# Second attention of a two-layer encoder: values stationary, split probabilities moving, and one part buffer less

## The chip, the cores and the metric

The kernel runs on one core of a Trainium2 chip. The metric is the device time of one execution in microseconds (us). Before the change it was 1018.17 us, the median of three runs (1017.5, 1018.17 and 1019.22).

## What is computed

An encoder of two layers on a sequence of 256 tokens with 1024 features, all in fp32. Each layer is a half-weighted feed-forward, an attention and a second half-weighted feed-forward, with a norm ahead of and behind each:

```python
for i in range(DEPTH):
    g = norm_g[i]
    h = h + FFN_RES * _rmsnorm(_swiglu(_rmsnorm(h, g[0]), ffn1_wg[i], ffn1_wu[i], ffn1_wd[i]), g[1])
    u = _rmsnorm(h, g[2])
    m = _diff_attention(...) if i == 0 else _neighborhood_attention(u, na_w_in[j], na_w_out[j], na_rpb[j])
    h = h + _rmsnorm(m, g[3])
    h = h + FFN_RES * _rmsnorm(_swiglu(_rmsnorm(h, g[4]), ffn2_wg[i], ffn2_wu[i], ffn2_wd[i]), g[5])
```

The feed-forward is `(silu(x @ wg) * (x @ wu)) @ wd` with 2816 inner features. The second attention has 16 heads of 64 features; the tokens are a grid of 4 rows of 64, each query sees the 16 columns of its window in all four rows, and a learned bias is added to the scores before the softmax:

```python
sc = jnp.einsum('bqhd,brqjhd->bhqrj', q_row, k_win).astype(jnp.float32) * scale
sc = sc + bias.astype(jnp.float32)[None]
p = jax.nn.softmax(sc.reshape(b, nh, GRID_W, kh * kw), axis=-1)
return jnp.einsum('bhqrj,brqjhd->bqhd', p, v_win)
```

## The kernel before, in words

Most products are done in three parts: an fp32 number is split into a high part, rounded to the type float32r, and a low part, the rest; a product is high times high, high times low and low times high, added up in PSUM.

**Weights.** The weights come in parts of 128x1024 numbers through SyncE's queue into four raw buffers (L106). ACT writes the high part `whi` (L130) and DVE the low part `wlo` (L131), each in two pieces of 512 columns, into part buffers, of which there are nine for each kind (L35, L160). `W.get` (L138) splits up to four parts ahead of the one asked for, but no more than nine past the oldest part that is not yet released; `W.release` (L145) comes behind the last product that uses a part.

**Stages.** Six follow one another: feed-forward, first attention (`diff` true), feed-forward, feed-forward of layer 1, second attention (`diff` false), feed-forward. The 256 tokens are two halves, t = 0 and 1. A feed-forward begins with row products (`proj_rows`, L376: 16 matmuls at L380 and L381, which alternate between whi and wlo of the four parts, then eight at L383 with whi; tokens stationary, 512 weight columns moving), goes on with column products (`proj_col`, L405) and down projections (`row_steps`, L421), and ends with four pairs of down projections, eight parts, first for t = 0, then for t = 1. An attention ends with the output projection, eight parts too. Between the two halves of that end stand the norms of t = 0 (`norms`, L315), and the next stage's first products run while DVE, ACT and POOL do the norms of t = 1. Their result xg is transposed by PE, four 128x128 transposes for each half of the features, and split into xT (`norm_T`, L371). In every stage but the very first feed-forward, both halves are transposed behind the second row product (L528, L746).

**The second attention.** v is projected by rows (`v_rows`, L561) and kept in fp32; q and k are projected by rows and transposed (`qk_rows`, `qk_T`) or by columns (`qk_cols`, L607), and split. Everything comes in two groups g of eight heads, two query halves qh and two sets pr of four heads. `scores` (L623) makes the scores in two PSUM banks; `softmax` (L637) adds the bias on DVE (L652), takes the exponential on ACT (L661) and keeps 1/sum in `rz`. `probs_T` (L677) transposes the probabilities, 16 transposes for a g, qh and pr in two banks, and copies one bank with ACT (L684) and one with DVE (L686). `av` (L690) multiplies them by v in fp32: probabilities stationary, 64 columns of v moving (L702); DVE scales the result by `rz` (L710). `o_T` (L732) transposes that result and splits it into oT, which the output projection `wout` (L740) uses. The order of the calls is written out from L744 on; a scheduler then places the instructions on the engines, with a head start of 100 for `split_bank` (L349) and 200 for `norms`.

In PSUM there are four banks `acc`, two `mm` and two `tr`.

Of the kernel before, what the change touches and what calls it, by code (L numbers as in the profile page):

```python
# [34 lines left out]
PART_BUFS = 9  # L35
# [116 lines left out]
def encoder_kernel(ctx, tc, x, norm_g, f1g, f1u, f1d, f2g, f2u, f2d,  # L152
# [9 lines left out]
    l4p = ctx.enter_context(tc.tile_pool(name="l4p", bufs=6))  # L162
# [208 lines left out]
    def norm_T(xg, xT, t):  # L371
        for b in range(2):
            k = slice(4 * b, 4 * b + 4)
            transpose_split(xg[b], xT[0][:, t, k, :], xT[1][:, t, k, :])

    def proj_rows(ps, xT, t, keys):  # L376
        parts = [W.get(key) for key in keys]
        w = [(wh[:, j, :], wl[:, j, :]) for wh, wl in parts for j in range(wh.shape[1])]
        for kt, (wh, wl) in enumerate(w):
            nc.tensor.matmul(ps, xT[0][:, t, kt, :], wh, start=kt == 0, stop=False)  # L380
            nc.tensor.matmul(ps, xT[0][:, t, kt, :], wl, start=False, stop=False)  # L381
        for kt, (wh, wl) in enumerate(w):
            nc.tensor.matmul(ps, xT[1][:, t, kt, :], wh, start=False, stop=kt == KT - 1)  # L383
        if t == NH - 1:
            for key in keys:
                W.release(key)
# [84 lines left out]
    def ffn(key, li, gpre, xg1, xT, gpost, last, aside=None):  # L471
# [3 lines left out]
        def gu_rows(nme, t):  # L475
            ps = mm_tile()
            proj_rows(ps, xT, t, [(key, nme, 0, j) for j in range(KT * NC // UE)])
# [74 lines left out]
    def attn(key, li, gpre, xg1, xT, gpost):  # L552
# [8 lines left out]
        def v_rows(g, t):  # L561
            ps = mm_tile()
            proj_rows(ps, xT, t, keys_of(2, g))
            if t == 0:
                vv[g] = vp.tile([P, NH, NC], F32, tag="v", name=nm("v"))
            nc.scalar.activation(vv[g][:, t, :], ps, AF.Copy)
# [13 lines left out]
        def qk_rows(part, g, t):  # L580
            ps = mm_tile()
            proj_rows(ps, xT, t, keys_of(part, g))
# [54 lines left out]
        def softmax(g, qh, pr, banks):  # L637
# [26 lines left out]
            if diff:  # L664
# [7 lines left out]
                ps = ps[:1]  # L672
            steps[g, qh, pr] = ps, rz
# [3 lines left out]
        def probs_T(g, qh, pr):  # L677
            ps, rz = steps.pop((g, qh, pr))
            res = []
            for c, p in enumerate(ps):  # L680
# [8 lines left out]

        def av(g, qh):  # L690
            ob = bank(ps_tr, "tr")
            o = t2p.tile([P, NC], F32, tag="t2", name=nm("o"))
            e = P if diff else 64
            rzs = []
            for pr in range(2):
                aT, rz = aTs.pop((g, qh, pr))
                rzs.append(rz)
                for j in range(2):
                    for c in range(len(aT)):
                        hd = (2 * pr + j) if diff else (4 * pr + 2 * j + c)  # L700
# [4 lines left out]
                if not diff:  # L705
                    s = slice(pr * 256, (pr + 1) * 256)
                    l = [list(v_) for v_ in rz.ap]
                    rzb = bass.AP(tensor=rz.tensor, offset=rz.offset,
                                  ap=[l[0], [l[2][0], 2], [l[1][0], 2], [0, e]])
                    nc.vector.tensor_tensor(out=o[:, s].rearrange("p (j c e) -> p j c e", j=2, c=2),  # L710
                                            in0=ob[:, s].rearrange("p (j c e) -> p j c e", j=2, c=2),
                                            in1=rzb, op=ALU.mult)
            if diff:
                f = 1.0 - LAM_INIT
                ss = sm.tile([P, 4], F32, tag="ss4", name=nm("ss4"))
                for hd in range(4):
                    square(ob[:, hd * P:(hd + 1) * P], rzs[hd // 2][:, 0, hd % 2:hd % 2 + 1], ss[:, hd:hd + 1])
                ms = sm.tile([P, 4], F32, tag="ms", name=nm("sub"))
                nc.vector.tensor_scalar(out=ms, in0=ss, scalar1=1.0 / (P * f * f), scalar2=EPS / (f * f),
                                        op0=ALU.mult, op1=ALU.add)  # L720
                rs = sm.tile([P, 4], F32, tag="rs", name=nm("sub"))
                nc.gpsimd.tensor_tensor(out=rs, in0=ms, in1=mhalf, op=ALU.pow)
                for pr in range(2):
                    nc.vector.tensor_tensor(out=rs[:, 2 * pr:2 * pr + 2], in0=rs[:, 2 * pr:2 * pr + 2],
                                            in1=rzs[pr][:, 0, :], op=ALU.mult)
                for hd in range(4):
                    s = slice(hd * P, (hd + 1) * P)
                    nc.vector.scalar_tensor_tensor(out=o[:, s], in0=ob[:, s], scalar=rs[:, hd:hd + 1],
                                                   in1=subg, op0=ALU.mult, op1=ALU.mult)
            return o  # L730

        def o_T(g, qh, o):  # L732
            tr = transposes(o)
            hi, lo = [v[:, qh, 4 * g:4 * g + 4, :] for v in oT]
            if not diff:
                hi, lo, tr = [v.rearrange("p j (r q) -> p (j r) q", q=GRID_W) for v in (hi, lo, tr)]
                tr = flip(tr)
# [7 lines left out]
        qk_rows(0, 0, 0)  # L745
        norm_T(xg1, xT, 1)  # L746
# [25 lines left out]
        W.extra(len(W.extras))  # L772
        scores(0, 0, 0)
        scores(0, 0, 1)
        if diff:
            qk_rows(0, 1, 1)
            qk_T(0, 1, 0)
        else:
            qk_cols(0, 1)
        scores(0, 1, 0)  # L780
        probs_T(0, 0, 0)
        scores(0, 1, 1)
        probs_T(0, 0, 1)
        if not diff:
            queue_bias(1)
        o = av(0, 0)
        if diff:
# [4 lines left out]
        else:  # L792
            qk_cols(1, 1)
        o_T(0, 0, o)
        probs_T(0, 1, 0)
        probs_T(0, 1, 1)
        o = av(0, 1)
        if diff:
# [89 lines left out]
```

## Time and profile before

| | |
|---|---|
| timed runs, median | 1018.17 us |
| profiled execution | 1021.54 us |
| its span, first to last instruction | 1019.8 us |
| mean granted clock of TensorE | 0.997 of full speed |
| TensorE (PE) busy | 998.6 us, 98% |
| VectorE (DVE) busy | 661.4 us, 65% |
| ScalarE (ACT) busy | 579.1 us, 57% |
| GpSimd (POOL) busy | 22.9 us, 2% |
| HBM | 178 GB/s over the span |

Matmul records overlap, since they are pipelined: what a matmul costs PE is the distance from its start to the next one's start, not its duration. PEld is the load of the stationary operand, which runs beside the matmuls. The granted clock is 1.00 where TensorE has its full 2.4 GHz and 0.50 where it has 1.2 GHz.

### The profile page before, as it was taken

What the parts mean: (1) busy time and instruction counts of PE and PEld (TensorE: products, weight loads), DVE (VectorE), ACT (ScalarE), POOL (GpSimd) and SP (SyncE); (2) the same over time, 40 slices, a digit from 0 to 9 for tenths busy, and PEclk for the clock granted to TensorE, in tenths of its full rate; (3) what the DMA queues carried; (4) which work ended last, traced back from release to release, by engine and by line L of the source; (5) the groups of instructions that cost most, each with busy time, mean ns of one, the idle gap of its engine ahead of it and who ended that gap; (6) DMA issues with size and microseconds to landing.
All of it is one profiled execution on the core that took longest, in us unless ns stands there. A gap on an engine that the chain in (4) does not pass through costs nothing.

```text
span 1019.8 us, 14658 instructions
## 1 busy us (share of the span) xinstructions
PE 998.6 (98%) x5342; PEld 845.1 (83%) x5342; DVE 661.4 (65%) x1240; ACT 579.1 (57%) x1235; POOL 22.9 (2%) x38
## 2 busy tenths in 40 slices
PE   8899999999999999999999999999999999999997
PEld 5788888888777788888888888888898878888885
DVE  5666656577777666657576676657765477566562
ACT  6555555566776565555456555645755366555551
POOL 1000000000001000000000000000000010000000
PEclk9999999999999999999999999999999999999999
DMA  8866666375524766665377677546743446666631
GB/s 272 258 197 189 186 201 186 115 243 167 165 84 135 228 214 187 187 197 182 115 235 244 187 200 221 189 124 207 231 119 101 124 144 219 195 187 186 202 108 42
DMA packets 120825, 182.84 MB, mean 179 GB/s; under 512 B 5729, under 2 KB 87649, under 8 KB 120754
## 3 DMA queue, kind: packets, MB, share of 16 engines
q1 hardware_dynamic: 120608, 181.65, 57.6%
q8 instruction: 42, 0.69, 0.3%
q0 software_dynamic: 144, 0.26, 0.2%
q14 instruction: 29, 0.24, 0.1%
q10 hardware_dynamic: 2, 0.00, 0.0%
HBM read 180.84 MB, written 1.05 MB: 178 GB/s over the span
## 4 chain that ended last, share of the span: by engine, by line
PE 85%; DMA 4%; DVE 4%; ACT 4%; issue 1%; POOL 1%; SPq 0%; DVEq 0%; POOLq 0%; ACTq 0%
PE mm L413 25%; PE acc L438 24%; PE mm L415 13%; PE mm L380 5%; PE mm L381 5%; PE mm L383 4%; PE mm L438 2%; PE tr L702 2%; DVE wlo L131 2%; PE tr L365 2%; DMA raw<-in_ffn_wg_dram 2%; ACT whi L130 2%; DMA raw<-in_ffn_wu_dram 2%; DMA raw<-in_na_w_in_dram 1%; PE mm L397 1%
## 5 line engine op out<-in xcount | busy, mean ns | idle before, releaser
L131 DVE TENSOR_TENSOR wlo<-raw,whi 128x512 fp32r<-128x512 f32 x656 | 421.7, 686 | 201.5 <-ACT whi L130 114.4
L130 ACT ACTIVATE whi<-raw 128x512 fp32r<-128x512 f32 x656 | 365.6, 622 | 181.4 <-PE acc L438 51.2
L413 PE MATMUL mm<-xT,whi 128*128 128x512 f32 x1152 | 288.2, 392 | 0.7 <-DVE g L498 0.7
L413 PEld LDWEIGHTS mm<-xT,whi 128*128 128x128 f32 x1152 | 208.8, 189 | 40.1 <-DVE g L498 1.5
L438 PE MATMUL acc<-whi,hT 128*128 128x512 f32 x704 | 197.0, 391 | 0.0
L415 PEld LDWEIGHTS mm<-xT,wlo 128*128 128x128 f32 x1152 | 157.1, 190 | 11.3
L415 PE MATMUL mm<-xT,wlo 128*128 128x256 f32 x1152 | 160.6, 282 | 0.0
L438 PEld LDWEIGHTS acc<-whi,hT 128*128 128x128 f32 x704 | 130.3, 188 | 25.4
L380 PE MATMUL mm<-whi,xT 128*128 128x512 f32 x272 | 110.5, 406 | 3.7 <-ACT xT L355 3.4
L438 PE MATMUL acc<-wlo,hT 128*128 128x512 f32 x352 | 111.2, 390 | 0.0
L381 PE MATMUL mm<-wlo,xT 128*128 128x512 f32 x272 | 108.8, 400 | 0.1
L438 PEld LDWEIGHTS acc<-wlo,hT 128*128 128x128 f32 x352 | 66.1, 188 | 14.1
L383 PE MATMUL mm<-whi,xT 128*128 128x512 f32 x272 | 67.4, 390 | 0.0
L380 PEld LDWEIGHTS mm<-whi,xT 128*128 128x128 f32 x272 | 52.0, 191 | 16.8 <-ACT xT L355 6.0
L381 PEld LDWEIGHTS mm<-wlo,xT 128*128 128x128 f32 x272 | 51.9, 191 | 12.6 <-DVE wlo L131 2.6
L383 PEld LDWEIGHTS mm<-whi,xT 128*128 128x128 f32 x272 | 51.1, 188 | 10.6
L355 ACT ACTIVATE hT<-a 128x512 fp32r<-128x512 f32 x36 | 22.8, 633 | 63.7 <-DVE a L487 63.7
L498 DVE TENSOR_TENSOR u<-mm,u 128x256 f32<-128x256 f32 x72 | 30.4, 422 | 27.4 <-ACT u L497 27.2
L497 ACT ACTIVATE u<-mm 128x256 f32<-128x256 f32 x72 | 26.8, 373 | 29.6 <-PE mm L415 29.6
L497 ACT ACTIVATE g<-mm 128x256 f32<-128x256 f32 x72 | 26.7, 371 | 23.4 <-PE mm L415 23.4
L498 DVE TENSOR_TENSOR g<-mm,g 128x256 f32<-128x256 f32 x72 | 30.3, 420 | 10.2 <-ACT g L497 10.2
L330 DVE TENSOR_TENSOR yg<-acc,gain 128x512 f32<-128x512 f32 x20 | 13.7, 687 | 34.0 <-ACT junk L282 33.9
(113 smaller groups left out, 826.5 us busy)
## 6 DMA issues: line engine op xcount, KB each, us to landing
raw<-in_ffn_wg_dram SPq DMA_DIRECT2D x88, 512.0 KB, 4.6
raw<-in_ffn_wu_dram SPq DMA_DIRECT2D x88, 512.0 KB, 4.3
raw<-in_ffn_wd_dram SPq DMA_DIRECT2D x88, 512.0 KB, 4.0
raw<-in_diff_w_in_dram SPq DMA_DIRECT2D x24, 512.0 KB, 4.7
raw<-in_na_w_in_dram SPq DMA_DIRECT2D x24, 512.0 KB, 4.7
gain<-in_norm_g_dram SPq DMA_DIRECT2D x11, 512.0 KB, 5.1
raw<-in_diff_w_out_dram SPq DMA_DIRECT2D x8, 512.0 KB, 3.8
raw<-in_na_w_out_dram SPq DMA_DIRECT2D x8, 512.0 KB, 4.5
```

Source lines behind the costliest of these rows:

```text
L130: nc.scalar.activation(hi[:, e], raw[:, e], AF.Copy)
L131: nc.vector.tensor_tensor(out=lo[:, e], in0=raw[:, e], in1=hi.bitcast(F32)[:, e], op=ALU.subtract)
L355: last_act[0] = nc.scalar.activation(hi, ps, AF.Copy)
L365: nc.tensor.transpose(tr[:, j * P:(j + 1) * P], src[:, j * P:(j + 1) * P], ident)
L380: nc.tensor.matmul(ps, xT[0][:, t, kt, :], wh, start=kt == 0, stop=False)
L381: nc.tensor.matmul(ps, xT[0][:, t, kt, :], wl, start=False, stop=False)
L383: nc.tensor.matmul(ps, xT[1][:, t, kt, :], wh, start=False, stop=kt == KT - 1)
L413: nc.tensor.matmul(ps, wh, xT.both(kt), start=kt == 0, stop=False)
L415: nc.tensor.matmul(ps[:, S:], wl, xT.one(0, kt), start=False, stop=kt == KT - 1)
L438: nc.tensor.matmul(ys[b], (xh, xl)[xp](i), parts[i][wp][:, 0, HALVES[b]], start=first and b not in seen, stop=last and left[b] == 0)
L497: nc.scalar.activation(y[:, f], ps[:, S:], AF.Copy)
L498: nc.vector.tensor_tensor(out=y[:, f], in0=ps[:, :S], in1=y[:, f], op=ALU.add)
```

## The change

1. `PART_BUFS` goes from 9 to 8, and the pool `l4p`, which holds q, k, the split probabilities and the feed-forward's hidden parts, from 6 to 8 buffers.
2. `proj_rows` takes hooks: a function to call behind its n-th matmul. `while_rows` uses them to issue the first half of `norm_T` behind the 21st of 24 matmuls and the second half behind the 24th. This replaces the two halves behind the product in both attentions and in three feed-forwards.
3. In the second attention v is split into a high and a low part. The probabilities are scaled by 1/sum before they are transposed (32 instructions on DVE, 128x256), and the transposed ones are split, 16 banks, in the order of the mirrored columns. `av_cols` takes v as the stationary operand (64 columns) and the split probabilities of both query halves as the moving one (256 columns), 24 matmuls for each g and pr. The result has features on partitions and is split straight into oT; `o_T` and the scaling by `rz` fall away there. Its banks are of the kind `acc`.
4. The order of calls in the second attention is new: scores, transposes and values go by sets of heads, both query halves of a set behind one another.

```diff
-PART_BUFS = 9
+PART_BUFS = 8
...
-    l4p = ctx.enter_context(tc.tile_pool(name="l4p", bufs=6))
+    l4p = ctx.enter_context(tc.tile_pool(name="l4p", bufs=8))
...
+    def while_rows(xg, xT, t):
+
+        n = 3 * KT
+        return {n - 3: lambda: norm_T(xg, xT, t, [0]), n: lambda: norm_T(xg, xT, t, [1])}
+
+    def proj_rows(ps, xT, t, keys, hooks={}):
+
+        count = [0]
+
+        def product(*a, **k):
+            m = nc.tensor.matmul(*a, **k)
+            count[0] += 1
+            if count[0] in hooks:
+                with tc.issue_after(m.ins):
+                    hooks[count[0]]()
...
-            a0 = gated(gu_rows("u", 0), s0)
-            norm_T(xg1, xT, 1)
+            a0 = gated(gu_rows("u", 0, while_rows(xg1, xT, 1)), s0)
             s1 = act(gu_rows("g", 1))
...
+                vv[g] = [vp.tile([P, NH, NC], F32R, tag="v", name=nm("v")) for _ in range(2)]
+            split_bank(vv[g][0][:, t, :], vv[g][1][:, t, :], ps)
...
+            else:
+                for c in range(2):
+                    for j in range(2):
+                        nc.vector.tensor_scalar(out=ps[c][:, j, :], in0=ps[c][:, j, :],
+                                                scalar1=rz[:, c, j:j + 1], scalar2=None, op0=ALU.mult)
...
+            if not diff:
+                for c, p in enumerate(ps):
+                    if qh == 0:
+                        aTs[g, pr, c] = [l4p.tile([P, NH, 4, P], F32R, tag="l4", name=nm("aT")) for _ in range(2)]
+                    hi, lo = [v[:, qh].rearrange("p i (r q) -> p (i r) q", q=GRID_W) for v in aTs[g, pr, c]]
+                    tr = transposes(flat(p)).rearrange("p i (r q) -> p (i r) q", q=GRID_W)
+                    split_bank(hi, lo, flip(tr))
+                return
...
+        def av_cols(g, pr):
+
+            ob = [bank(ps_acc, "acc") for _ in range(2)]
+            aT = [aTs.pop((g, pr, c)) for c in range(2)]
+            vh, vl = vv[g]
+            for j in range(2):
+                for i, (w, a) in enumerate([(w, a) for w, a in ((vh, 0), (vh, 1), (vl, 0)) for _ in range(NH)]):
+                    kt = i % NH
+                    for c in range(2):
+                        hd = 4 * pr + 2 * j + c
+                        nc.tensor.matmul(ob[c][:64, j * S:(j + 1) * S],
+                                         w[:, kt, hd * 64:(hd + 1) * 64], aT[c][a][:, :, j * NH + kt, :],
+                                         start=i == 0, stop=i == 3 * NH - 1)
+            k = slice(4 * g + 2 * pr, 4 * g + 2 * pr + 2)
+            for c in range(2):
+                split_bank(*[v[c * 64:(c + 1) * 64, :, k, :].rearrange("p t k q -> p k t q") for v in oT],
+                           ob[c][:64].rearrange("p (k t q) -> p k t q", k=2, q=P))
...
-        qk_rows(0, 0, 0)
-        norm_T(xg1, xT, 1)
+        qk_rows(0, 0, 0, while_rows(xg1, xT, 1))
...
+        scores(0, 0, 0)
+        scores(0, 1, 0)
+        qk_cols(0, 1)
+        scores(0, 0, 1)
+        scores(0, 1, 1)
+        queue_bias(1)
+        probs_T(0, 0, 0)
+        probs_T(0, 1, 0)
+        qk_cols(1, 1)
+        av_cols(0, 0)
+        probs_T(0, 0, 1)
+        probs_T(0, 1, 1)
+        W.extra(len(W.extras))
+        scores(1, 0, 0)
+        scores(1, 1, 0)
+        av_cols(0, 1)
+        v_rows(1, 0)
+        scores(1, 0, 1)
+        scores(1, 1, 1)
+        v_rows(1, 1)
+        y0 = [mm_tile() for _ in range(2)]
+        probs_T(1, 0, 0)
+        probs_T(1, 1, 0)
+        wout(y0, 0, [0, 1, 2, 3])
+        av_cols(1, 0)
+        probs_T(1, 0, 1)
+        probs_T(1, 1, 1)
+        wout(y0, 0, [4, 5])
+        av_cols(1, 1)
```

Three pieces of the order follow. In the names, the number behind `whi`, `wlo` and `raw` is that of the part; parts 234 to 237 are those of the second row product of the second attention, and lines of the changed kernel are counted in its own file.

DVE, from layer 1's first feed-forward into the second attention, before:

```order
L131 TENSOR_TENSOR wlo236_6818<-raw236_6749,whi236_6817 128x512 x2
L131 TENSOR_TENSOR wlo237_6826<-raw237_6757,whi237_6825 128x512
L294 SCALAR_TENSOR_TENSOR pre_569_6787<-ss2_568_6782 128x1
L131 TENSOR_TENSOR wlo237_6826<-raw237_6757,whi237_6825 128x512
L307 SCALAR_TENSOR_TENSOR xg_571_6791<-h1_92,pre_570_6789,gain_447_5021 128x512
L307 SCALAR_TENSOR_TENSOR xg_572_6793<-h1_92,pre_570_6789,gain_447_5021 128x512
L131 TENSOR_TENSOR wlo238_6861<-raw238_6807,whi238_6860 128x512 x2
```

and of the changed kernel:

```order
L131 TENSOR_TENSOR wlo235_6810<-raw235_6715,whi235_6809 128x512 x2
L131 TENSOR_TENSOR wlo236_6818<-raw236_6749,whi236_6817 128x512
L294 SCALAR_TENSOR_TENSOR pre_569_6787<-ss2_568_6782 128x1
L131 TENSOR_TENSOR wlo236_6818<-raw236_6749,whi236_6817 128x512
L307 SCALAR_TENSOR_TENSOR xg_571_6791<-h1_92,pre_570_6789,gain_447_5021 128x512
L307 SCALAR_TENSOR_TENSOR xg_572_6793<-h1_92,pre_570_6789,gain_447_5021 128x512
L356 TENSOR_TENSOR v_578_6858<-mm_576_6800,v_577_6857 128x512
L131 TENSOR_TENSOR wlo237_6826<-raw237_6757,whi237_6825 128x512 x2
```

Part 236 has the place that part 237 had, and part 237 that of part 238, behind both xg; the low part of v is new ahead of it.

PE at the end of the same row product, where before the rows L365 stood behind all eight of the last matmuls; changed kernel:

```order
L386 MATMUL mm_579_6861<-wlo237_6826,xT_560_6676 128x512
L386 MATMUL mm_579_6861<-whi234_6801,xT_560_6676 128x512 x2
L386 MATMUL mm_579_6861<-whi235_6809,xT_560_6676 128x512 x2
L386 MATMUL mm_579_6861<-whi236_6817,xT_560_6676 128x512
L365 MATMUL tr_580_6883<-ident_116,xg_571_6791 128x128 x4
L386 MATMUL mm_579_6861<-whi236_6817,xT_560_6676 128x512
L386 MATMUL mm_579_6861<-whi237_6825,xT_560_6676 128x512 x2
L365 MATMUL tr_581_6893<-ident_116,xg_572_6793 128x128 x4
```

The first set of transposes of xg moved ahead of the product's last three matmuls.

PE where the first products with the values of the changed kernel's second set of heads end and the next row product begins:

```order
L732 MATMUL acc_670_7722<-aT_646_7621,v_577_6857 64x256 x2
L732 MATMUL acc_670_7722<-aT_647_7622,v_577_6857 64x256 x2
L732 MATMUL acc_670_7722<-aT_646_7621,v_578_6858 64x256 x2
L732 MATMUL acc_670_7722<-aT_646_7621,v_577_6857 64x256 x2
L732 MATMUL acc_670_7722<-aT_647_7622,v_577_6857 64x256 x2
L732 MATMUL acc_670_7722<-aT_646_7621,v_578_6858 64x256 x2
L386 MATMUL mm_672_7752<-whi250_7451,xT_560_6676 128x512
```

Here `v_577` and `v_578` are the high and the low part of v, `aT_646` and `aT_647` those of the probabilities; before, L702 had the fp32 probabilities and v here, with 64 columns to a matmul.

## Rows read from the trace of the kernel before

**Rows 1.** The page, part 1: busy us, share of the span, instructions.

```profile
PE 998.6 (98%) x5342; PEld 845.1 (83%) x5342; DVE 661.4 (65%) x1240; ACT 579.1 (57%) x1235; POOL 22.9 (2%) x38
```

**Rows 2.** Waits of PE and PEld, whole span: us in total, times, longest.

```profile
PE mm L380 <- ACT xT L355: 3.4, 6, 2.1
...
PE acc L632 <- ACT qk L355: 0.8, 1, 0.8
...
PE acc L633 <- DVE qk L356: 0.5, 1, 0.5
...
PEld mm L381 <- DVE wlo L131: 2.6, 7, 0.5
```

**Rows 3.** Timeline into the first attention: start us, us, engine, line, operation, count.

```profile
211.60 0.39 PE L381 MATMUL mm<-wlo,xT 128*128 128x512 f32 x1
...
211.82 1.98 PE L383 MATMUL mm<-whi,xT 128*128 128x512 f32 x8
212.96 1.28 DVE L131 TENSOR_TENSOR wlo<-raw,whi 128x512 fp32r<-128x512 f32 x2
...
213.64 1.04 PE L365 MATMUL tr<-ident,xg 128*128 128x128 f32 x8
...
214.98 0.50 PE L380 MATMUL mm<-whi,xT 128*128 128x512 f32 x1 [0.30 <-ACT xT L355]
```

**Rows 4.** Timeline of PE, second attention, transposes of nat between two products.

```profile
713.12 0.60 PE L365 MATMUL tr<-ident,nat 128*128 128x128 f32 x4
713.47 0.48 PE L380 MATMUL mm<-whi,xT 128*128 128x512 f32 x1
713.78 0.39 PE L381 MATMUL mm<-wlo,xT 128*128 128x512 f32 x1
```

**Rows 5.** Timeline, into the second feed-forward.

```profile
331.24 1.89 DVE L131 TENSOR_TENSOR wlo<-raw,whi 128x512 fp32r<-128x512 f32 x3
...
331.98 0.50 PE L381 MATMUL mm<-wlo,xT 128*128 128x512 f32 x1
```

**Rows 6.** Timeline, into layer 1.

```profile
518.22 0.39 PE L381 MATMUL mm<-wlo,xT 128*128 128x512 f32 x1
...
519.35 1.29 DVE L131 TENSOR_TENSOR wlo<-raw,whi 128x512 fp32r<-128x512 f32 x2
```

**Rows 7.** Timeline, into the second attention.

```profile
704.02 0.50 PE L381 MATMUL mm<-wlo,xT 128*128 128x512 f32 x1
...
705.74 1.28 DVE L131 TENSOR_TENSOR wlo<-raw,whi 128x512 fp32r<-128x512 f32 x2
```

**Rows 8.** Timeline, into the last feed-forward.

```profile
834.84 2.49 DVE L131 TENSOR_TENSOR wlo<-raw,whi 128x512 fp32r<-128x512 f32 x4
...
836.18 0.50 PE L381 MATMUL mm<-wlo,xT 128*128 128x512 f32 x1
```

**Rows 9.** Timeline of PE, second attention's end: its first and last rows.

```profile
730.54 0.60 PE L365 MATMUL tr<-ident,nat 128*128 128x128 f32 x4
...
827.07 0.40 PE L380 MATMUL mm<-whi,xT 128*128 128x512 f32 x1
```

**Rows 10.** Timeline of PE, second attention: q and k projection by columns, values.

```profile
754.24 0.28 PE L398 MATMUL mm<-xT,whi 128*128 128x256 f32 x1
754.36 0.28 PE L399 MATMUL mm<-xT,wlo 128*128 128x256 f32 x1
754.50 2.00 PE L702 MATMUL tr<-v,aT 128*128 128x64 f32 x16
756.31 0.36 PE L397 MATMUL mm<-xT,whi 128*128 128x256 f32 x1
```

**Rows 11.** Windows: length, busy PE, PEld, DVE, ACT, POOL; then PEclk, DMA, GB/s.

```profile
33.00:36.00 3.00, 0.40 (x3) 0.05 (x1) 2.00 (x4) 2.30 (x4) 0.00 (x0) 1.00 0.78 269
734.00:738.00 4.00, 4.00 (x26) 3.78 (x25) 3.83 (x20) 3.51 (x9) 0.00 (x0) 0.57 0.38 135
730.00:827.00 97.00, 94.16 (x658) 82.40 (x658) 58.94 (x156) 53.83 (x138) 1.42 (x2) 0.98 0.38 115
```

More of the change, by code (lines that the diff above doesn't have):

```diff
@@ L379, in proj_rows @@
         for kt, (wh, wl) in enumerate(w):
-            nc.tensor.matmul(ps, xT[0][:, t, kt, :], wh, start=kt == 0, stop=False)
-            nc.tensor.matmul(ps, xT[0][:, t, kt, :], wl, start=False, stop=False)
+            product(ps, xT[0][:, t, kt, :], wh, start=kt == 0, stop=False)
+            product(ps, xT[0][:, t, kt, :], wl, start=False, stop=False)
         for kt, (wh, wl) in enumerate(w):
-            nc.tensor.matmul(ps, xT[1][:, t, kt, :], wh, start=False, stop=kt == KT - 1)
+            product(ps, xT[1][:, t, kt, :], wh, start=False, stop=kt == KT - 1)
         if t == NH - 1:
@@ L473, in ffn, with gu_rows @@
         hT = {}
-        def gu_rows(nme, t):
+        def gu_rows(nme, t, hooks={}):
             ps = mm_tile()
-            proj_rows(ps, xT, t, [(key, nme, 0, j) for j in range(KT * NC // UE)])
+            proj_rows(ps, xT, t, [(key, nme, 0, j) for j in range(KT * NC // UE)], hooks)
             return ps
@@ L692, in av @@
             o = t2p.tile([P, NC], F32, tag="t2", name=nm("o"))
[L693 removed]
+            e = P
             rzs = []
@@ L704, in av @@
                                              start=kt == 0, stop=kt == NH - 1)
[L705 to L729, printed above, removed]
+            f = 1.0 - LAM_INIT
@@ new lines, in av @@
+            ss = sm.tile([P, 4], F32, tag="ss4", name=nm("ss4"))
+            for hd in range(4):
+                square(ob[:, hd * P:(hd + 1) * P], rzs[hd // 2][:, 0, hd % 2:hd % 2 + 1], ss[:, hd:hd + 1])
+            ms = sm.tile([P, 4], F32, tag="ms", name=nm("sub"))
+            nc.vector.tensor_scalar(out=ms, in0=ss, scalar1=1.0 / (P * f * f), scalar2=EPS / (f * f),
+                                    op0=ALU.mult, op1=ALU.add)
+            rs = sm.tile([P, 4], F32, tag="rs", name=nm("sub"))
@@ new lines, in av @@
+            nc.gpsimd.tensor_tensor(out=rs, in0=ms, in1=mhalf, op=ALU.pow)
+            for pr in range(2):
+                nc.vector.tensor_tensor(out=rs[:, 2 * pr:2 * pr + 2], in0=rs[:, 2 * pr:2 * pr + 2],
+                                        in1=rzs[pr][:, 0, :], op=ALU.mult)
+            for hd in range(4):
+                s = slice(hd * P, (hd + 1) * P)
+                nc.vector.scalar_tensor_tensor(out=o[:, s], in0=ob[:, s], scalar=rs[:, hd:hd + 1],
+                                               in1=subg, op0=ALU.mult, op1=ALU.mult)
@@ new lines, in attn @@
+            wout(y0, 0, [0, 1, 2, 3])
+            probs_T(1, 0, 0)
+            probs_T(1, 0, 1)
+            o = av(1, 0)
+            y1 = [bank(ps_acc, "acc") for _ in range(2)]
+            wout(y1, 1, [0, 1])
+            probs_T(1, 1, 0)
+            probs_T(1, 1, 1)
+            o_T(1, 0, o)
+            o = av(1, 1)
+            wout(y0, 0, [4, 5])
+            wout(y0, 0, [6, 7])
+            xg = norms(0, y0, gpost, gpre, False)
+            o_T(1, 1, o)
+            wout(y1, 1, [2, 3])
@@ L795, in attn @@
+            wout(y1, 1, [4, 5, 6])
+            nxT = xt_tiles("xT")
+            norm_T(xg, nxT, 0)
+            wout(y1, 1, [7])
+            xg = norms(1, y1, gpost, gpre, False)
+            return xg, nxT
+        W.extra(len(W.extras))
+        scores(0, 0, 0)
+        scores(0, 1, 0)
+        qk_cols(0, 1)
+        scores(0, 0, 1)
+        scores(0, 1, 1)
+        queue_bias(1)
+        probs_T(0, 0, 0)
         probs_T(0, 1, 0)
+        qk_cols(1, 1)
+        av_cols(0, 0)
+        probs_T(0, 0, 1)
```

65 lines of the change are left out of this document (23 added, 42 removed).

## The prediction, made before the changed kernel ran

> **What bounds the kernel now.** I read the page's busy times first, then the list of what TensorE waits for, then the timeline around each place that the change touches. PE is busy for 998.6 us, 98% of the span [rows 1], and the longest entry among its waits is 3.4 us in total [rows 2]. So the time is PE's own stream: a microsecond that PE is spared, or waits, is one of the run, and DVE (65%) and ACT (57%) matter only where PE arrives before their result. I therefore go along PE's stream and ask what gets shorter and what comes late. The profiled execution took 1021.54 us, the timed runs have a median of 1018.17; differences are worked out in the trace and put on the median. Under 0.2%, about 2 us, a measurement of this kernel cannot be told from no change.
>
> **Transposes inside a product (a gain).** At five places PE did both sets of transposes of xg behind the product and then waited for ACT's split. At the first, the product ends at 213.64 and the next begins at 214.98: 1.34 us [rows 3]; the other four show the same rows with 1.29 or 1.34, together 6.55 us. Now the first set stands three matmuls ahead of the product's end, and its split runs beside those. Eight 512-column matmuls take 211.82 to 213.64, 0.23 us each [rows 3]. One set between matmuls, with the slower first matmul behind it, takes from 713.12 to 713.78 [rows 4]; less that matmul's 0.23, a set costs 0.43 us. Two sets at five places make 4.3 us, a gain of 6.55 - 4.3 = **2.2 us**. The wait for the split, 0.30 us in the row of 214.98, goes in any case, so at least 1.4 us.
>
> **Nine part buffers to eight (a loss).** A feed-forward and an attention end with eight parts held to their last products. With nine buffers one part of the next stage could be split ahead of them; with eight none can. The order on DVE shows what that does: around the boundary each part's wlo stands where the following part's stood. Raw loads shift alike, since a raw buffer comes free with its split. So I take the time at which the following part's second half was done, and compare it with the start of the matmul that needs the part last with wlo, the sixteenth of the stage's second product:
> - into the first attention, wlo ends at 212.96 + 1.28 = 214.24, that matmul stood at 211.60: 2.6 us [rows 3];
> - into the feed-forward behind it, 331.24 + 1.89 = 333.13 against 331.98: 1.2 us [rows 5];
> - into layer 1, 519.35 + 1.29 = 520.64 against 518.22: 2.4 us [rows 6];
> - into the second attention, 705.74 + 1.28 = 707.02 against 704.02, and the new split of v with 0.6 us (half of the 1.28 for two wlo) stands ahead of it: 3.6 us [rows 7];
> - into the last feed-forward, 834.84 + 2.49 = 837.33 against 836.18: 1.2 us [rows 8].
>
> In sum **11.0 us**. The reason is that wlo of the product's last part is now queued behind both xg of the norm, which in the trace it preceded. Behind the waiting matmul PE has only its own next products, whose parts are then ready, so nothing is lost twice. Elsewhere the trace shows reserve: PE's weight loads wait for a wlo at L381 alone, seven times and 2.6 us in all [rows 2], and never in the column products or the down projections. There I put the loss of a buffer at nothing; the cover is parts split ahead, and if it is gone, each late part costs up to one half split, 0.6 us. Ends: 8 us, if two of the smaller places turn out covered, and 13 us, if ACT's half, also shifted, is late on top.
>
> **The end of the second attention (a gain).** From the transposes of nat at 730.54 to the next stage's first product at 827.07 it takes 96.5 us [rows 9].
> - Values: 128 records with 64 columns, 16 of them from 754.50 to 756.31, 0.11 each: some 14.2 us. In their place come 96 matmuls with 256 moving columns; the nearest rows, 256 columns of the same class of operands, are 0.12 us apart (754.24, 754.36) [rows 10]: 11.5 us. Ends: 0.11, the record replaced, and 0.23, the 512-column step [rows 3]: 10.6 to 22 us. I stay at 0.12, since the columns are the same number. Gain 2.7.
> - Four sets of transposes of o go: 4 x 0.43 = 1.7 us.
> - Clock: from 734 to 738 the granted clock was 0.57, so half speed for most of it: 4 x 0.43 = 1.7 us lost [rows 11], right behind PE's waits for qk of 0.8 and 0.5 us [rows 2]. Before that place stand now 19 matmuls whose data are done, 12 of scores and 7 of the next projection, so I take the 1.7 us as gained.
> - Waits: 0.8 and 0.5 for qk [rows 2], and some shorter ones for aT. After: the scores of the second query half need q's second half, split in the same places of ACT and DVE as what PE waited for before, so the same 1.3 us; and where the scores of group 1 begin, two splits of oT and two of aT stand on DVE ahead of a bank that the next transposes need, some 1.0 us. I put the difference at 0.
> - Smaller pieces of PE's time between kinds of work: the values' matmuls were cut into the projections in pieces (754.36, 754.50 and 756.31 are such changes [rows 10]), o's transposes into other products. Each such change costs some 0.08 us, which is what the set of transposes shows, 0.31 us from 713.47 to 713.78 for a matmul of 0.23 [rows 4], and some 20 go: 1.6 us.
>
> Together 2.7 + 1.7 + 1.7 + 1.6 = **7.7 us**. What hides the rest: 32 new scalings of 128x256, 16 splits of p in place of 8 copies, four of v and four more of oT keep DVE busy for some 16 us more, at 0.3 us for 256 columns and 0.6 for 512 by the same pair of wlo, less 3 us for eight scalings that go. DVE had 58.9 us in 97 [rows 11] and gets about 75 in 89: still covered, except in bursts such as the 1.0 us above. Ends: 4.5 us, with 3.5 us more of such waits, and 10.5 with none.
>
> **Sum.** -2.2 + 11.0 - 7.7 = +1.1 us: 1018.17 + 1.1, rounded **1019.0 us**, no change.
>
> **Rivals.**
> - *Slower: the clock falls at the boundaries.* PE's waits there come in pieces with two matmuls between, as ahead of 734. Against it: the 3 us from 33 to 36, with 0.40 us of PE work in them, kept the clock at 1.00 [rows 11]. If each of the three long waits (2.4 to 3.6 us) costs 1.7 us, as from 734 to 738, that is 5.1: 1024.1 us. It decides from one fall on: 1019.0 + 1.7 = 1020.7 us. The Trainium skill, "TensorE: Matmul & The Clock Gate", Part 1, says that the gate follows how busy PE has recently been and that half speed is the state after idleness; by that rule each boundary wait is a candidate. The fall behind 734 agrees with it, the stretch from 33 to 36 does not. Chance 0.22.
> - *Slower: DVE fills up.* With 4.5 in place of 7.7 us from the attention's end: 1022.5 us. For it: the 75 of 89 us. Against: most of it lies beside the projections of q and k, which ask nothing of DVE. Chance 0.10.
> - *Faster: the buffers cost half.* If the scheduled place is not what bounds wlo, because parts that stood later in the order were simply not wanted earlier, 11.0 becomes 4 to 6: 1012 to 1014 us. Against: DVE works its queue in order, and xg ahead of the part are bound by the norm. Chance 0.24. If eight buffers cost nothing, so that the change only does its other parts: 1018.2 - 9.9 = 1008 us, chance 0.08.
>
> **How the numbers follow.** The forecast, within 2 us of no change, has 0.36, faster 0.24 + 0.08 = 0.32, slower 0.22 + 0.10 = 0.32. All losses high and gains low give 1018.2 - 1.4 + 13 - 4.5 = 1025.3; with a fall of the clock beside it the range reaches 1026. Losses low and gains high give 1013.5; half-price buffers with the best gains reach 1010. Range 1010 to 1026.
>
> **What would show it.** In the second product of each stage the last matmuls with wlo should wait for DVE, by 2.6, 1.2, 2.4, 3.6 and 1.2 us more than before; without these waits the buffer term is wrong. Behind that product no more than 0.5 us should stand until the next. The values' matmuls should be 0.12 us apart. From the transposes of nat to the next stage some 89 us should stand in place of 96.5. A clock under 1.00 behind a boundary would be the first rival, more than 5 us of waits of PE for aT, oT or p from DVE the second.

## The result, and the profile after

| | before | after |
|---|---|---|
| timed runs, median of 8 each | 1018.91 us | 1024.24 us |
| ratio, with its 95% interval | | 1.0057, 1.0042 to 1.0072 |
| profiled execution | 1021.54 us | 1024.0 us |
| its span | 1019.8 us | 1022.2 us |

The kernel became slower by 0.57%, 5.8 us by the ratio (the two medians lie 5.3 us apart), where the prediction had 1019.0 us, no change, as the likeliest outcome. The time lies inside the stated range of 1010 to 1026 us, at the place of its first rival. PE does less and still ends later: the page's first part, after, to be held against [rows 1]:

```profile
PE 994.6 (97%) x5294; PEld 839.8 (82%) x5294; DVE 676.6 (66%) x1280; ACT 586.3 (57%) x1247; POOL 22.6 (2%) x38
```

PE has 4 us less of busy time, and more waits. The waits of PE and PEld over the whole span (us in total, times, longest), after, to be held against [rows 2]; lines 380 and 381 of the old file are L386 here:

```profile
PE mm L386 <- DVE wlo L131: 8.1, 6, 2.3
PE mm L386 <- ACT xT L355: 2.1, 2, 1.9
...
PE tr L365 <- DVE aT L356: 1.5, 2, 0.8
...
PE acc L651 <- ACT qk L355: 0.8, 1, 0.8
PE mm L453 <- DVE v L356: 0.8, 1, 0.8
...
PE mm L453 <- ACT oT L355: 0.3, 1, 0.3
```

```profile
PEld mm L386 <- DVE wlo L131: 16.0, 23, 2.8
```

The wait of the weight loads for wlo grew from 2.6 us [rows 2] to 16.0. In the matmuls themselves it is 8.1 us, where the kernel before shows no wait of a matmul for wlo over 0.15 us in these places. The five boundaries have one long one each. Timeline of PE after, start and length in us, with the idle time before it in brackets; in order into the first attention, the second feed-forward, layer 1, the second attention and the last feed-forward:

```profile
212.03 0.50 PE L386 MATMUL mm<-wlo,xT 128*128 128x512 f32 x1 [1.72 <-DVE wlo L131]
...
332.17 0.50 PE L386 MATMUL mm<-wlo,xT 128*128 128x512 f32 x1 [0.54 <-DVE wlo L131]
...
521.64 0.64 PE L386 MATMUL mm<-wlo,xT 128*128 128x512 f32 x1 [1.73 <-DVE wlo L131]
...
712.13 0.50 PE L386 MATMUL mm<-wlo,xT 128*128 128x512 f32 x1 [2.32 <-DVE wlo L131]
...
839.12 0.50 PE L386 MATMUL mm<-wlo,xT 128*128 128x512 f32 x1 [1.59 <-DVE wlo L131]
```

In four of them it is the fourteenth matmul of the product that waits, in the second feed-forward the twelfth: the first half of the product's last part (there the half before it) came late already, not only the second half, which the sixteenth needs and which the prediction looked at. Matmuls near the wait also stand 0.33 us apart in place of 0.23:

```profile
212.63 0.50 PE L386 MATMUL mm<-wlo,xT 128*128 128x512 f32 x1
212.96 1.32 PE L386 MATMUL mm<-whi,xT 128*128 128x512 f32 x5
```

Into the second attention the wait is 0.6 us longer than into the first; there the new split of v stands on DVE between xg and wlo:

```profile
709.46 1.41 DVE L307 SCALAR_TENSOR_TENSOR xg<-h,pre,gain 128x512 f32<-128x512 f32 x2 [0.45 <-POOL pre L297]
710.79 0.68 DVE L356 TENSOR_TENSOR v<-mm,v 128x512 fp32r<-128x512 f32 x1
711.39 1.28 DVE L131 TENSOR_TENSOR wlo<-raw,whi 128x512 fp32r<-128x512 f32 x2
```

The row at 521.64 differs in its length, 0.64 us against 0.50: there the clock has fallen. Windows after (length, busy PE, PEld, DVE, ACT, POOL; then granted clock, DMA share, GB/s), all of 5 us up to PE's last matmul whose clock is under 0.985:

```profile
520.00:525.00 5.00, 3.36 (x8) 2.48 (x9) 2.19 (x4) 0.00 (x0) 0.00 (x0) 0.69 0.91 295
525.00:530.00 5.00, 5.00 (x27) 4.17 (x26) 1.89 (x3) 1.20 (x2) 0.00 (x0) 0.97 0.30 102
...
710.00:715.00 5.00, 2.87 (x8) 2.09 (x9) 2.67 (x5) 0.00 (x0) 0.00 (x0) 0.80 0.81 260
715.00:720.00 5.00, 5.00 (x25) 4.16 (x24) 1.38 (x2) 1.68 (x3) 0.00 (x0) 0.86 0.30 107
```

A clock of 0.69 over 5 us is 5 x 0.31 = 1.55 us lost, with 0.15 in the next window 1.7 in all; the second pair gives 1.0 + 0.7 = 1.7. These are two falls, both behind a boundary's wait, of the three that the first rival spoke of.

To see where all of the time lies, I cut PE's timeline of each run at the same places: for a boundary, from the first matmul of the next stage's first product to the first of its third, which holds the wait, the transposes and any fall of the clock. In us, profiled executions:

| boundary into | before | after | less the fall | change | predicted (wait less 0.44 of hooks) |
|---|---|---|---|---|---|
| first attention | 12.22 | 14.33 | 14.33 | +2.1 | 2.6 - 0.44 = +2.2 |
| second feed-forward | 12.71 | 12.96 | 12.96 | +0.25 | 1.2 - 0.44 = +0.8 |
| layer 1 | 12.17 | 16.09 | 14.4 | +2.2 | 2.4 - 0.44 = +2.0 |
| second attention | 12.50 | 17.06 | 15.4 | +2.9 | 3.6 - 0.44 = +3.2 |
| last feed-forward | 12.58 | 13.73 | 13.73 | +1.15 | 1.2 - 0.44 = +0.8 |
| sum | 62.18 | 74.17 | 70.8 | +8.6 | +8.8 |

The rest of the second attention, from its third product to its end, went from 119.53 to 111.68 us, 7.85 less (predicted 7.7). Part of that is chance: the execution before had a fall of the clock in this stretch, 1.7 us, that is no work of the change (below). The stretch, after, is shown by its first and last rows, to be held against [rows 9]:

```profile
740.28 0.60 PE L365 MATMUL tr<-ident,nat 128*128 128x128 f32 x4
...
828.98 0.39 PE L386 MATMUL mm<-whi,xT 128*128 128x512 f32 x1
```

The last stage is 0.6 us shorter behind its boundary, and the other stretches changed by less than 0.3 us each, but for the start: the first stage took 202.76 us before and 201.27 after, and between 199.5 and 203.8 in all the runs below, in no order of buffers or hooks; in three of them a fall of the clock is in it. What sets the rest of it was not looked into. So the two spans differ by only 2.5 us; with the fall (1.7) and the longer start (1.5) of the execution before set aside it is 5.7, near the timed 5.8.

The end of the second attention, windows (same columns, to be held against the last of [rows 11]) and groups by line (engine, operation, out<-in, count, busy us, mean ns, idle before), after:

```profile
740.00:829.00 89.00, 85.50 (x609) 75.82 (x608) 72.50 (x192) 59.22 (x147) 1.10 (x2) 1.00 0.37 117
```

```profile
L732 PE MATMUL acc<-aT,v 128*64 128x256 f32 x96 | 11.9, 278 | 0.0
L671 DVE CUSTOM_DVE_ANT_0 p<-acc,bias 128x256 f32<-128x256 f32 x32 | 11.9, 418 | 0.0
...
L356 DVE TENSOR_TENSOR aT<-tr,aT 128x512 fp32r<-128x512 f32 x16 | 10.7, 687 | 1.6 <-ACT aT L355 1.3
...
L695 DVE TENSOR_SCALAR p<-p,rz 128x256 f32<-128x256 f32 x32 | 9.1, 349 | 0.2
...
L356 DVE TENSOR_TENSOR oT<-acc,oT 64x512 fp32r<-64x512 f32 x8 | 5.5, 683 | 5.5 <-ACT oT L355 5.3
```

DVE is busy for 72.5 of 89 us, near the forecast's 75, and PE waits for it only twice for aT and once for v, 2.3 us in all: the second rival did not come. All waits of PE in the stretch, 2.6 us before, are 3.4 after; the forecast had no difference. The clock is 1.00 throughout.

### The profile page after: what moved, and what is told of

It is laid out like the page before. It is cut to its first block, busy times and chain, and to the rows that moved or that the text cites. A ratio compares the mean times of both kernels' runs of the same rounds, so it can differ in the third digit from the quotient of the medians.

```text
span 1022.2 us, 14601 instructions
## 1 busy us (share of the span) xinstructions
PE 994.6 (97%) x5294; PEld 839.8 (82%) x5294; DVE 676.6 (66%) x1280; ACT 586.3 (57%) x1247; POOL 22.6 (2%) x38
## 4 chain that ended last, share of the span: by engine, by line
PE 79%; DVE 7%; DMA 5%; ACT 5%; issue 3%; POOL 1%; SPq 0%; POOLq 0%; DVEq 0%; ACTq 0%
PE mm L428 26%; PE acc L453 21%; PE mm L430 13%; PE mm L386 11%; DVE wlo L131 3%; DMA raw<-in_ffn_wu_dram 3%; PE mm L453 2%; PE tr L365 2%; ACT whi L130 2%; ACT junk L282 1%; ACT p L680 1%; PE acc L732 1%; PE tr L752 1%; POOL pre L297 1%; PE mm L413 1%
## 5 line engine op out<-in xcount | busy, mean ns | idle before, releaser
L386 PE MATMUL mm<-whi,xT 128*128 128x512 f32 x544 | 180.2, 404 | 2.2 <-ACT xT L355 2.1
L386 PEld LDWEIGHTS mm<-whi,xT 128*128 128x128 f32 x544 | 104.4, 193 | 23.8 <-ACT xT L355 3.3
L386 PE MATMUL mm<-wlo,xT 128*128 128x512 f32 x272 | 110.8, 407 | 8.1 <-DVE wlo L131 8.1
L386 PEld LDWEIGHTS mm<-wlo,xT 128*128 128x128 f32 x272 | 52.0, 191 | 25.5 <-DVE wlo L131 16.0
L282 ACT ACTIVATE junk<-acc 128x512 bf16<-128x512 f32 x20 | 11.8, 591 | 39.1 <-PE acc L453 39.1
L355 ACT ACTIVATE xT<-tr 128x512 fp32r<-128x512 f32 x24 | 13.6, 594 | 34.4 <-PE tr L365 34.4
```

The lines of the kernel that those rows point to most:

```text
L282: nc.scalar.activation(junk[:, :n], src, AF.Square, scale=scale, accum_out=acc)
L355: last_act[0] = nc.scalar.activation(hi, ps, AF.Copy)
L386: m = nc.tensor.matmul(*a, **k)
```

## The experiments

Theory A is the forecast's buffer term: eight buffers put wlo of the product's last part behind both xg on DVE at each boundary. Theory C is the first rival: the clock falls behind those waits and adds to them. All ratios are to the kernel before on the same chip; the expectations stand as they were put down before each run.

**Eight buffers alone.** The kernel before, with one number changed:

```diff
-PART_BUFS = 9
+PART_BUFS = 8
```

> The kernel before with PART_BUFS = 8 and nothing else. Theory A (the boundaries): each of five boundaries loses what the following part's split is late, 2.6 + 1.2 + 2.4 + 3.6 - 0.6 (no v split here) + 1.2 = 10.4 us, and one to three falls of TensorE's clock at 1.7 us come on top: 12 to 16 us over the kernel before, some 1030 to 1035 us; the matmuls with wlo wait 7 us or more in total. Rival B (the attention): the new attention costs the time by itself and eight buffers are nearly free: no more than 3 us over the kernel before.

Measured: 1028.94 us against 1018.52, ratio 1.0099 (1.0081 to 1.0117), some 10 us. The boundaries sum to 75.2 us against 62.18, with three falls of the clock in it. Windows of this run (columns as above):

```profile
210.00:215.00 5.00, 4.08 (x10) 3.08 (x11) 1.47 (x3) 0.00 (x0) 0.00 (x0) 0.66 0.88 315
520.00:525.00 5.00, 3.94 (x11) 2.91 (x12) 1.61 (x3) 0.00 (x0) 0.00 (x0) 0.71 0.84 281
710.00:715.00 5.00, 3.28 (x11) 2.23 (x10) 2.52 (x4) 0.00 (x0) 0.00 (x0) 0.83 0.90 271
```

and its timeline into the first attention, which shows the queue on DVE: xg, then the late wlo, then the matmul that waited:

```profile
208.85 1.42 DVE L307 SCALAR_TENSOR_TENSOR xg<-h,pre,gain 128x512 f32<-128x512 f32 x2 [0.44 <-POOL pre L297]
210.18 1.29 DVE L131 TENSOR_TENSOR wlo<-raw,whi 128x512 fp32r<-128x512 f32 x2
...
210.92 0.50 PE L381 MATMUL mm<-wlo,xT 128*128 128x512 f32 x1 [1.72 <-DVE wlo L131]
```

So the buffer alone makes the loss. The order xg, then wlo is the same at the other four boundaries of this run. Without the falls (3 x 1.7) the boundaries cost 75.2 - 5.1 - 62.18 = 7.9 us.

**Eight buffers and hooks,** without the new attention: the edit above, with `while_rows` and the hooks of the change.

> The kernel before with PART_BUFS = 8 and with the transposes of xg inside the product, the old attention kept. Theory A: 2.2 us less than with eight buffers alone, so 10 to 14 us over the kernel before, and 6 to 8 us slower than the changed kernel, the difference being what the new attention gains. Rival B: within 2 us of the kernel before, the changed kernel being the slower one.

Measured: 1031.51 us, ratio 1.0121 (1.0096 to 1.0147). Its interval overlaps the one of eight buffers alone: the 2.2 us of the hooks are not to be seen here. In the traces the boundaries without the falls sum to 70.1 us without hooks and 69.6 with them, while PE's waits for wlo grew from 6.0 to 6.7 us. The changed kernel is this one plus the new attention (and the `l4p` buffers), and is faster by 1.0121 - 1.0057 = 0.64%, 6.5 us.

**The wait filled.** The changed kernel, with seven matmuls whose result nobody reads behind the thirteenth of the second product, at four of the boundaries (not the second feed-forward's). The late wlo remains; PE works while it waits.

```diff
+    def fill(xT, n):
+        ps = bank(ps_tr, "tr").rearrange("p (j q) -> p j q", q=P)
+        for _ in range(n):
+            nc.tensor.matmul(ps, xT[0][:, 0, 0, :], xT[0][:, 0, 0:4, :], start=True, stop=True)
...
+        if busy:
+            hooks[13] = lambda: fill(xT, busy)
```

> The changed kernel with seven matmuls of 512 columns more, 1.6 us of work that nothing reads, in the longest wait of four of the boundaries (behind the 13th matmul of the second product, where TensorE waits 1.9 to 2.5 us). Theory C (the clock falls because TensorE stands still at the boundary): the granted clock stays at 1.00 behind the boundaries into layer 1 and into the second attention, and the time falls by 3 us to some 1021 us, although more is computed. Rival D (the clock falls there for another reason, or its fall costs nothing): the clock falls as before, and the time is that of the changed kernel or up to 2 us more.

Measured: 1023.07 us, ratio 1.0036 (1.0020 to 1.0052). The seven matmuls into the first attention, and the windows behind the three long waits of this run:

```profile
212.23 1.75 PE L379 MATMUL tr<-xT 128*128 128x512 f32 x7
```

```profile
210.00:215.00 5.00, 4.86 (x20) 3.02 (x19) 4.23 (x8) 1.24 (x4) 0.93 (x1) 1.00 0.73 250
520.00:525.00 5.00, 4.88 (x19) 3.25 (x19) 3.25 (x6) 0.00 (x0) 0.86 (x1) 1.00 0.92 310
710.00:715.00 5.00, 4.31 (x18) 2.91 (x18) 3.22 (x5) 0.00 (x0) 0.10 (x1) 1.00 0.88 290
```

No fall at any boundary; they sum to 71.2 us, what the changed kernel has without its two falls (70.8). In the times the gain, 0.0057 - 0.0036 = 0.21%, has the right sign and two thirds of the size, but the two intervals overlap. The granted clock of the timed executions decides it: its mean is 0.9945 over the eight of the changed kernel and 0.9972 over these twelve, 5.6 and 2.8 us lost (what is missing from 1.00, times the span). Each of these losses holds 1 to 2.4 us (in the profiled executions) behind PE's last matmul, where nothing is lost by it.

This trace also has a fall in the first stage, at PE's wait for `a`, and so has the next run's. It is the stretch from 33 to 36 us in which the prediction saw the clock stay at 1.00 [rows 11]. The wait filled, then the late splits sooner:

```profile
35.00:40.00 5.00, 4.74 (x17) 3.95 (x18) 0.90 (x2) 0.60 (x1) 0.00 (x0) 0.67 0.37 140
```

```profile
35.00:40.00 5.00, 5.00 (x18) 3.97 (x17) 0.73 (x2) 1.00 (x3) 0.00 (x0) 0.75 0.28 93
```

**The late splits sooner.** The changed kernel, with a head start of 240 in the scheduler for the splits of the four parts of the second products:

```diff
+            with self.tc.high_priority(offset=EARLY_BY) if i in EARLY else nullcontext():
```

> The changed kernel with a head start of 240 in the scheduler for the splits of the four parts of every second product, so that their wlo stand ahead of the norm's pre and xg on DVE; eight buffers as before. Theory E (the loss comes from the place in DVE's queue, behind xg): the waits for wlo fall from 8.1 us to under 4, the clock does not fall at the boundaries, and the time is 6 to 9 us less than the changed kernel's, 1015 to 1018 us. Rival F (the buffer itself, its raw load or the norm, is late): the wait moves to wlo's raw data or to xg, and no more than 2 us are gained.

Measured: 1023.42 us, ratio 1.0038 (1.0020 to 1.0057). The waits of PE in this run, and the matmul into the first attention:

```profile
PE mm L389 <- DVE xT L359: 6.1, 3, 2.1
```

```profile
211.47 2.02 PE L389 MATMUL mm<-whi,xT 128*128 128x512 f32 x4 [2.07 <-DVE xT L359]
```

The wait moved from the weights to the norm's xT, whose splits now stood behind the pulled ones, and at three boundaries it was as long (2.07, 2.02 and 2.05 us). The clock fell behind it too, at two boundaries (0.66 from 210 to 215). The boundaries sum to 70.8 us with these two falls and 67.4 without, 3.4 less than after the change and 8.7 more than with nine buffers (below). So the place in the queue is worth about a quarter of the loss when it is bought in this way, and theory E's 6 to 9 us did not come; what binds the rest, beyond DVE's own work at the boundary, was not separated. The timed gain, 0.19%, has overlapping intervals.

**Hooks alone.** The kernel before with nine buffers and its attention, and `while_rows`.

> The kernel before, nine part buffers and the old attention, with the transposes of xg inside the product and nothing else. Theory H (the term of the prediction): five gaps of 1.3 us behind the second products become two separate sets of transposes, 2.2 us less, some 1016 us, and the stretch from a stage's start to its third product shrinks by 0.4 us at each of the five. Rival I (the runs with eight buffers showed no gain from it): the stretch keeps its length because xg or its split comes late, under 0.5 us in all.

Measured: 1016.57 us against 1019.77, ratio 0.9966 (0.9949 to 0.9984). The boundaries sum to 60.26 us, 1.9 less than before: four of them shrank by 0.5 to 0.9 us, and the first attention's grew by 0.5, where PE waited 0.64 us for a wlo. So the term is about right where the buffers are nine.

**Nine buffers kept.** The changed kernel, with `l4p` at 6 to pay for the ninth part buffer:

```diff
-PART_BUFS = 8
+PART_BUFS = 9
...
-    l4p = ctx.enter_context(tc.tile_pool(name="l4p", bufs=8))
+    l4p = ctx.enter_context(tc.tile_pool(name="l4p", bufs=6))
```

> The changed kernel with PART_BUFS = 9 again, the memory for it taken from l4p, six buffers in place of eight, so that in the second attention some splits of q, k and of the probabilities wait for a buffer. Theory A (the boundaries): the waits for wlo at the boundaries shrink to what they were before, under 3 us in all, and the clock does not fall there: 9 + 3 us less at the boundaries, 1 to 4 us more inside the second attention, so 1013 to 1017 us, faster than the kernel before. Rival B (the attention): the time stays above 1021 us.

Measured: 1012.37 us, ratio 0.9918 (0.9892 to 0.9943): faster than both kernels, and a little under the 1013 to 1017 us expected. The weight loads' wait for wlo, of the 16.0 us after, is in this run

```profile
PEld mm L386 <- DVE wlo L131: 0.2, 1, 0.2
```

and its boundary into the second attention goes through at full clock (same columns as above):

```profile
700.00:710.00 10.00, 10.00 (x51) 8.32 (x51) 6.38 (x11) 4.32 (x9) 0.34 (x1) 1.00 0.62 206
```

The boundaries sum to 58.7 us, 15.5 less than after; the rest of the attention took 112.97 in place of 111.68, 1.3 more with two `l4p` buffers fewer. 15.5 - 1.3 = 14.2 us is the difference of the times too: 1.0057 - 0.9918 = 1.39%, 14.2 us, give or take 3 by the two intervals.

**Nine buffers from elsewhere.** `PART_BUFS` 9, `l4p` 7 and three raw buffers in place of four:

> The changed kernel with PART_BUFS = 9, the memory for it taken from l4p (seven buffers) and from the raw buffers (three in place of four). Theory A: as with six l4p buffers at the boundaries, with less waiting inside the second attention; if three raw loads in flight are enough, 1011 to 1015 us. If they are not, TensorE waits for whi and wlo behind raw data in every stage and the time is above 1018 us.

Measured: 1031.33 us, ratio 1.0108 (1.0083 to 1.0133), the slowest but one. The waits of PE in this run:

```profile
PE mm L386 <- DVE wlo L131: 7.3, 5, 2.3
...
PE mm L386 <- ACT whi L130: 2.2, 1, 2.2
```

The wait for whi is a single one, in the first stage, and ACT itself had waited there for the raw data:

```profile
16.56 1.15 ACT L130 ACTIVATE whi<-raw 128x512 fp32r<-128x512 f32 x2 [3.23 <-DMA raw<-in_ffn_wg_dram]
```

At the boundaries one half of a wlo stayed behind xg, and PE waited 1.2 to 2.3 us at four of them. Without the falls they sum to 67.8 us, 3.0 less than after the change. But the run had as many falls of the clock as any other, two of them twice as long, and in time the ninth part buffer, paid with a raw buffer, was a loss.

**The attention alone.** Nine part buffers, `l4p` 6, no hooks:

```diff
-            a0 = gated(gu_rows("u", 0, while_rows(xg1, xT, 1)), s0)
+            a0 = gated(gu_rows("u", 0), s0)
+            norm_T(xg1, xT, 1)
...
-        qk_rows(0, 0, 0, while_rows(xg1, xT, 1))
+        qk_rows(0, 0, 0)
+        norm_T(xg1, xT, 1)
```

> The new attention alone: nine part buffers, six l4p buffers, the transposes of xg behind the product as before. If the three parts add up, the attention gains 4 to 6 us over the kernel before (its stretch was 4.8 us shorter with the transposes inside, in the trace of the kernel with nine part buffers), some 1013.5 to 1016 us, and this is 2 to 4 us slower than with the transposes inside the product. If the transposes inside are worth nothing beside the new attention, it equals that kernel, 1012 us.

Measured: 1014.52 us against 1020.29, ratio 0.9942 (0.9919 to 0.9964), so 5.9 us for the attention (3.7 to 8.3), as expected; its boundaries sum to 61.3 us, about what they take in the kernel before. It is 0.24%, 2.4 us, slower than with the transposes inside, also as expected, though the two intervals overlap.

**Values between the halves of k's projection.** The kernel with nine buffers and hooks, with the first values' matmuls in the middle of the last column projection:

```diff
-        qk_cols(1, 1)
+        qk_cols(1, 1, [0])
         av_cols(0, 0)
+        qk_cols(1, 1, [1])
```

> Nine part buffers, six l4p buffers, transposes inside; in the second attention av_cols(0, 0) stands between the two halves of qk_cols(1, 1), so that the l4p buffers come free before the splits of that projection want them. If the 1.3 us by which the attention's stretch was longer than with eight l4p buffers came from that wait, some 1 us less than with av_cols behind the projection, 1011.5 us; if they came from the waits of the second set of heads (probabilities for a free buffer), no difference, within 0.5 us.

Measured: 1010.11 us against 1020.29, ratio 0.9892 (0.9872 to 0.9912), the fastest of all. The interval overlaps with that of nine buffers without this edit, and its trace has a fall of the clock in the attention that the other lacks. With that fall taken off, the rest of the attention took 111.9 us, 1.1 less than there, which is the expected size; in the times it can't be told from nothing.

## Why the prediction was right in its range and wrong in its sum

**The transposes inside the product: right.** 2.2 us forecast; with nine buffers 1.9 us in the trace (hooks alone) and 61.3 - 58.7 = 2.6 (nine buffers with and without hooks), 0.45 to 0.64 at each of the five. From the second set to the third product 0.36 us stand after the change, within the 0.5 allowed:

```profile
215.24 0.60 PE L365 MATMUL tr<-ident,xg 128*128 128x128 f32 x4
215.60 0.48 PE L386 MATMUL mm<-whi,xT 128*128 128x512 f32 x1
```

With eight buffers the timed runs show none of it. The mean granted clock accounts for some: the six executions with hooks lost 7.2 us by it, the six without 5.7. The rest stays open.

**The buffer: right in mechanism and about right in size.** 11.0 us forecast, with ends of 8 and 13. Measured without falls, 7.9 (eight buffers alone), 9.3 (with hooks: 73.0 - 3.4 - 60.3) and 12.1 (after against nine buffers: 70.8 - 58.7). With the hooks' 0.44 taken off, each boundary came within 0.6 us of its term; the v split's 0.6 us is the difference of the waits into the second attention, 2.32 after and 1.72 with eight buffers alone. That wlo stands behind both xg on DVE is shown by the rows of eight buffers alone. The rival of half price, 4 to 6 us, is met by none of the three sums. That the place in the queue is the whole cause is not shown: with the splits pulled ahead of xg about three quarters of the loss stayed.

**The end of the second attention: the work about right, the clock wrong.** From the transposes of nat (740.28) to the next stage (828.98) it took 88.7 us; 89 were forecast. The values' matmuls stand some 0.114 us apart (0.12 forecast), and the scaling took 349 ns (0.3):

```profile
771.68 2.90 PE L732 MATMUL acc<-aT,v 128*64 128x256 f32 x24
```

The 1.6 us for smaller pieces and the 1.7 for o's transposes were not measured apart. But 1.7 of the 7.7 us were the fall from 734 to 738, counted as a gain of the change, so that 7.85 measured against 7.7 is in part luck. The old attention has no such fall in three other executions (eight buffers alone, with hooks, hooks alone), and the new one has it in three of its seven (late splits sooner, raw 3, values between halves). One window from the hooks alone, and one from the values between the halves:

```profile
735.00:740.00 5.00, 5.00 (x45) 5.00 (x43) 2.18 (x5) 4.04 (x12) 0.00 (x0) 1.00 0.29 105
```

```profile
735.00:740.00 5.00, 5.00 (x36) 5.00 (x35) 1.61 (x8) 2.02 (x9) 0.00 (x0) 0.77 0.25 88
```

So the old attention does not always have it, and the new one is not free of it. In these traces it goes with PE's wait for q and k just ahead. In the new attention that wait is 1.84 to 2.52 us in the three that fell and 0.84 to 1.51 in the four that did not; in the old one it is 0.82 and 0.46 in the one that fell, 0.57 and 0.46 or 0.46 alone in the others. The wait of the values between halves:

```profile
PE acc L652 <- ACT qk L355: 1.8, 1, 1.8
```

Without the fall, the old rest of the attention takes 117.0 to 117.8 us and the new one 111.7, a gain of about 5.7. With six `l4p` buffers, as in the attention alone, the new one takes 112.7, a gain of 4.3 to 5.1; the timed 5.9 there (3.7 to 8.3) does not contradict either. The profiled execution of before was 3.4 us above the median of the runs then shown; a loss in it that the other runs need not have was the place to be careful.

**The step that failed in the sum is the clock, twice.** I took it at 1.00 behind the boundaries, on the one stretch from 33 to 36 us [rows 11], where in two of the later traces it did fall, and left the falls to a rival with 0.22; in the attention I took a fall of one execution for a property of the kernel. Put right: +1.1, and 1.7 for the attention's fall that is no gain, and two falls of 1.7 at the boundaries: 1.1 + 1.7 + 3.4 = 6.2 us, against 5.8 measured (4.3 to 7.3 by the interval). So close an agreement is partly luck, since each term is uncertain by a microsecond or so. The first rival's mechanism decided, at its own price of 1.7 us for a fall, with two falls of its three in the profiled execution.

What bears the clock's part out: in the four profiled executions with eight buffers and nothing to fill the wait, it fell behind nine of the twelve boundaries into the first attention, layer 1 and the second attention, where the longest single waits are 1.7 to 2.3 us, and behind none of the eight boundaries of the two other feed-forwards (0.54 and 1.59 us after). With nine part buffers and four raw ones (before, hooks alone and the three kernels with `l4p` 6 and raw 4) it fell behind no boundary at all, and neither with the waits filled. The timed executions say the same: with eight buffers and nothing to fill the wait the mean granted clock costs 5.6 to 7.2 us of the span, with the waits filled 2.8, and with nine buffers and four raw ones 2.0 to 3.5 (2.3 to 2.9 in the kernel before). The Trainium skill, "TensorE: Matmul & The Clock Gate", Part 1, has the gate follow how busy PE has recently been. The falls behind the waits, and their absence where the waits are short or filled, agree with that, and it was the better guide than the single stretch from 33 to 36 us. Which of the waits brings a fall stays open: the same 1.72 us into the first attention brought one with eight buffers alone and none after the change.

## What to carry to other kernels

A buffer taken from a pool that feeds the bounding engine was paid here at every stage boundary: look there which piece of work moves behind which on the in-order queue that fills the buffers, and cost it from the end of that work to the start of its user. To a wait of about 2 us of TensorE in such a place add a likely fall of its clock, 1.7 us here behind nine of twelve. And before a loss in one profiled execution is counted as a gain, see how that execution stands to the median of the runs, and look for the same loss in a second trace; one stretch without a fall is no evidence against the falls either.

## What the hardware showed beyond this

- A single fall of the clock cost 1.7 us in three different places: 1.55 + 0.15 into layer 1, 1.0 + 0.7 into the second attention, and 1.7 in the attention's middle [rows 11]. With three raw buffers two falls lasted twice as long, 3.4 us each. One of them, behind the boundary into the second attention:

```profile
710.00:715.00 5.00, 2.68 (x9) 1.48 (x9) 4.12 (x8) 1.99 (x4) 0.86 (x1) 0.85 0.81 247
715.00:720.00 5.00, 5.00 (x17) 4.04 (x17) 1.52 (x3) 1.22 (x3) 0.00 (x0) 0.50 0.82 232
720.00:725.00 5.00, 5.00 (x23) 4.08 (x22) 0.69 (x1) 1.18 (x3) 0.00 (x0) 0.97 0.14 45
```

- Seven matmuls of 512 columns that nobody reads, 1.75 us, in a wait kept the clock at 1.00 behind the boundaries.
- The multiplication of 128x256 by a number per partition on DVE took 349 ns from SBUF to SBUF, against 418 for L671, which adds the bias to the scores in a PSUM bank and keeps their maximum, at the same size.
